# Merge gates of a hybrid decoder: seven products of block sums instead of eight block products

## The chip, the cores and the metric

The kernel runs on one core of a Trainium2 chip. Times are microseconds (us) of device time for one call; a call computes both layers. The median of three runs of the kernel before is 2449.65 us (2448.92 to 2451.15).

## The reference, cut to what matters

Two layers, 1024 prompt tokens and 8 sample tokens (T = 1032), model width 1024. Each layer makes four branch outputs y of width 384 and merges them:

```python
h = rms_norm(x, norm_g)                                   # (T, 1024)
proj_b = einsum('bsne,ned->bsnd', branches, w_branch)     # 4 x (384 -> 1024)
gates  = sigmoid(h @ w_merge)                             # 1024 -> 4 * 1024
merged = sum(gates * proj_b, over the 4 branches)
x = x + merged @ w_out
```

`h @ w_merge` is the largest product of the layer. Everything is float32 in and out.

## The kernel before, in words

Activations lie feature-major: 128 features by T tokens a tile, eight tiles k = 0..7 for the model width. Each fp32 operand is kept as a high and a low part (fp32r), and a product is three matmuls: high x high, high x low, low x high (`mm_cols`, L178, L181, L182). The normalised input is `hh` and `hl`. A weight tile arrives raw (`wr`), ScalarE (ACT) copies its high part `wh` (L154), GpSimd (POOL) subtracts to get the low part `wl` (L156); that is `split_w`. `wr` has 2 buffers, `wh` and `wl` 4 each, of up to 8 x 128 columns.

The merge of a layer (L884 to L923) loops over the four branches `bi`, over eight output tiles `m` and over three chunks of 344 tokens. For each it issues 24 gate matmuls (k = 0..7) and 9 matmuls of the branch projection, all of 344 columns. Then VectorE (DVE) scales the gate by 1/rms (`rr`, L917), ACT takes tanh (L918), DVE multiplies with the projection out of PSUM (L920, L922), and from the second branch on POOL adds it to the sum `mg` (L923). Per layer this is 4 x 8 x 3 x 33 = 3168 matmuls, 6336 in both. After it `mg` is split into parts (`split_m`, L881, L882) for the output projection (L983 on).

A scheduler of the framework puts each engine's instructions in order. Each engine then runs its own list strictly in order and waits on semaphores. Pools with a fixed number of buffers set when a tile can be written again. "Tag" below is such a set of buffers: `slot` has 31.

Of the kernel before, what the change touches and what calls it, by code (L numbers as in the profile page):

```python
# [7 lines left out]
F32 = mybir.dt.float32  # L8
F32R = mybir.dt.float32r
# [4 lines left out]
P = 128  # L14
# [6 lines left out]
NCH = 3  # L21
MIX = 384
# [10 lines left out]
def kernel(ctx: ExitStack, tc: tile.TileContext, i, o, c):  # L33
# [5 lines left out]
    sl = ctx.enter_context(tc.tile_pool(name="sl", bufs=31))  # L39
# [33 lines left out]
    # ---- loads are held back until the products a given number of tiles before them have been issued  # L73
# [23 lines left out]
    # ---- constants  # L97
# [17 lines left out]
    # ---- cache copies, cut in pieces that go out between the weights  # L115
# [32 lines left out]
    # ---- weights: raw tile -> high and low parts  # L148
    def split_w(shape, dmas):
        raw = wp.tile(list(shape), F32, tag="wr", name="wr", bufs=2)  # L150
# [4 lines left out]
        lo = wp.tile(list(shape), F32R, tag="wl", name="wl", bufs=4)  # L155
        pool.tensor_tensor(lo, raw, hi.bitcast(F32), op=ALU.subtract)  # L156
        return hi, lo

# [3 lines left out]
    def w_std(src, kt):  # L162
        r = split_w([P, kt, P], [(lambda t: t, src)])
        copy_piece()
        return r

    def w_pair(l, c0, j):
        r = split_w([P, KT, P], [
            (lambda t: t[:, :, 0:64], win_cols(l, c0 + 64 * j, 64)),
            (lambda t: t[:, :, 64:128], win_cols(l, c0 + 192 + 64 * j, 64))])  # L170
        copy_piece()
        return r

# [13 lines left out]
    # short products that go out one lot after each chunk of long ones  # L187
# [10 lines left out]
    # ---- the normalised input is kept as (x * g) in two parts; 1/rms is applied to what the products give  # L198
# [75 lines left out]
    for l in range(2):  # L274
        # ================= projections with rotary positions
# [21 lines left out]
        # ================= layer constants  # L297
# [42 lines left out]
        # ================= token-major projections  # L340
        def tm_group(srcs, kk, consumer):
            N = sum(n for _, n in srcs)
            ws = []
            for k0 in range(0, KT, kk):
# [7 lines left out]
                copy_piece()  # L352
# [18 lines left out]
        def tm_v(srcs, off):  # L371
            """V rows of two attentions: to memory, to the caches"""
# [9 lines left out]
            tm_group(srcs, 4, ev)  # L382
# [27 lines left out]
        tm_group([(C_V, MIX)], 2, ev_c)  # L410
# [17 lines left out]
        # ================= branch C: layer norm and spatial mix  # L428
# [82 lines left out]
        def pv(s, nk, vs, out):  # L511
            """vs[kb][h]: [128 keys, 64]; out: psum [128, 128] for the two heads."""
# [15 lines left out]
        # ---- branch B, prompt  # L528
# [35 lines left out]
        # ---- decode of both attention branches  # L564
        class Decode:
# [14 lines left out]
            def scores(self, j, q, k):  # L580
                """q, k: [128, 8], two heads of the new tokens"""
# [20 lines left out]
        def decode_finish(D, O):  # L602
# [47 lines left out]
            def values(j0):  # L650
                """two parts, one per head"""
# [33 lines left out]
        yscr = [dscr(f"yscr{l}_{n}", [3, P, T]) for n in range(3)]  # L685
# [5 lines left out]
        # ================= branch A  # L691
# [38 lines left out]
        # ---- branch D, prompt  # L730
# [85 lines left out]
        # ---- gates of B  # L816
# [13 lines left out]
        # ---- weights of the dilated groups from their maxima and denominators  # L830
# [48 lines left out]
        def split_m(m, ch):
            cs = slice(ch * CH, (ch + 1) * CH)  # L880
            act.activation(mh[m][:, cs], mg[m][:, cs], AF.Copy)  # L881
            dve.tensor_tensor(ml[m][:, cs], mg[m][:, cs], mh[m].bitcast(F32)[:, cs], op=ALU.subtract)  # L882

        order = (2, 3, 1, 0)  # L884
        for bi, n in enumerate(order):
            yh, yl = [], []
            yy = ynext
            for j in range(3):
                t = yy[j]
                th, tl = slot(f"yh{n}{j}", F32R), slot(f"yl{n}{j}", F32R)  # L890
                act.activation(th, t, AF.Copy)
                dve.tensor_tensor(tl, t, th.bitcast(F32), op=ALU.subtract)
                yh.append(th)
                yl.append(tl)
            for m in range(KT):
                ms = slice(m * P, (m + 1) * P)
                if n == 1:
                    wv = i["w_branch"][l, n, :, ms].rearrange("(h j p) m -> h p j m", h=2, p=64)
                    wpj = split_w([P, 3, P], [(lambda t: t[0:64], wv[0]), (lambda t: t[64:128], wv[1])])
                else:  # L900
                    wpj = split_w([P, 3, P], [(lambda t: t,
                                               i["w_branch"][l, n, :, ms].rearrange("(j p) m -> p j m", p=P))])
                wg = w_std(i["w_merge"][l, :, n * DM + m * P:n * DM + (m + 1) * P].rearrange("(k p) m -> p k m", p=P), KT)
                if bi == 0:
                    mg[m] = slot(f"mg{m}")
                if bi == 0 and m == 0:
                    ynext = yD
                if m == 4 and bi in (1, 2):
                    ynext = load_y(order[bi + 1])
                for ch in range(NCH):  # L910
                    cs = slice(ch * CH, (ch + 1) * CH)
                    pg = pacc()
                    mm_chunk(pg, wg, KT, hh, hl, ch)
                    pp = pacc()
                    mm_chunk(pp, wpj, 3, yh, yl, ch)
                    t = ctmp("th")
                    dve.tensor_tensor(t, pg[:, :CH], rr[:, cs], op=ALU.mult)  # L917
                    act.activation(t, t, AF.Tanh, scale=0.5)  # L918
                    if bi == 0:
                        dve.scalar_tensor_tensor(mg[m][:, cs], t, 1.0, pp[:, :CH], op0=ALU.add, op1=ALU.mult)  # L920
                    else:
                        dve.scalar_tensor_tensor(t, t, 1.0, pp[:, :CH], op0=ALU.add, op1=ALU.mult)  # L922
                        pool.tensor_tensor(mg[m][:, cs], mg[m][:, cs], t, op=ALU.add)  # L923
# [14 lines left out]
        def final_block(n, last):  # L938
            """final norm of one block of tokens, back to token-major"""
# [81 lines left out]
def _constants():  # L1021
    """Tables that depend on shapes alone: rotary factors by position, masks, the identity."""
# [35 lines left out]
```

## Time and profile before

| | |
|---|---|
| median of three runs | 2449.65 us |
| span of the profiled execution | 2449.6 us |
| busy: PE / DVE / ACT / POOL | 99% / 37% / 29% / 34% |
| granted TensorE clock, mean | 0.994 |
| DMA | 235.82 MB, mean 96 GB/s |

The span is the time from the first to the last instruction of the profiled execution, and it stands at the median of the timed runs, so a sum against the span is one against the median. PE is TensorE's matmuls; its busy share counts overlapping matmuls once.

### The profile page before, as it was taken

The page shows a single profiled execution, that of the slowest core. Times are in us where ns is not written, and L with a number is a line of the kernel's source. Part 1 is how long each engine was busy: PE and PEld are TensorE (multiplying, and loading weights), DVE is VectorE, ACT ScalarE, POOL GpSimd, SP SyncE. Part 2 cuts the span into 40 slices and gives each one's busy share as a digit, 9 for nine tenths or more (in the row PEclk, how much of TensorE's full clock was granted, in tenths as well). Part 3 has the DMA queues.
Part 4 walks back from the last instruction along what each step waited for, and adds up shares of the span by engine and source line. Part 5 has one row for each costly group of instructions (what it writes and reads, how often), then busy time and mean ns, then how long its engine had stood idle before and what let it go on. Part 6 is the DMA issues. An engine that isn't in the chain of part 4 may idle for free.

```text
span 2449.6 us, 38865 instructions
## 1 busy us (share of the span) xinstructions
PE 2423.4 (99%) x15896; PEld 2305.9 (94%) x15896; DVE 894.5 (37%) x1930; ACT 705.7 (29%) x1526; POOL 841.5 (34%) x556
## 2 busy tenths in 40 slices
PE   8999999999999999999999999999999999999999
PEld 7998889889999999999999988898899999999998
DVE  4456534435312221224333554443352122212253
ACT  6234432322212221224323254313222121212243
POOL 3342235342222343444433413343223233444330
PEclk9999999999999999999999999999999999999999
DMA  7252216242322222223442523342352221222232
GB/s 240 87 150 80 71 45 184 64 134 81 94 69 65 92 65 95 65 68 120 146 146 73 147 66 80 100 147 60 100 137 67 70 91 56 93 65 69 76 97 99
DMA packets 295963, 235.82 MB, mean 96 GB/s; under 512 B 52757, under 2 KB 279697, under 8 KB 293417
## 3 DMA queue, kind: packets, MB, share of 16 engines
q1 hardware_dynamic: 267952, 206.25, 28.1%
q10 hardware_dynamic: 27832, 27.10, 3.9%
q8 instruction: 125, 2.05, 0.4%
q14 instruction: 54, 0.43, 0.1%
HBM read 192.35 MB, written 76.47 MB: 110 GB/s over the span
## 4 chain that ended last, share of the span: by engine, by line
PE 94%; DVE 2%; DMA 1%; ACT 1%; POOL 1%; issue 0%; ACTq 0%; SPq 0%; POOLq 0%; DVEq 0%
PE acc L181 26%; PE acc L178 26%; PE acc L182 26%; PE sc L500 3%; PE acc L360 2%; PE acc L363 2%; PE acc L364 2%; PE ms L522 2%; PE ms L517 2%; PE ms L662 1%; DMA qs<-dk 1%; PE ms L467 0%; DVE ml L882 0%; DVE dk L291 0%; POOL qs L290 0%
## 5 line engine op out<-in xcount | busy, mean ns | idle before, releaser
L156 POOL TENSOR_TENSOR wl<-wr,wh 128x384 fp32r<-128x384 f32 (+2 forms) x228 | 465.9, 2045 | 864.5 <-ACT wh L154 764.7
L181 PE MATMUL acc<-h1l,wh 128*128 128x344 f32 x1584 | 513.7, 324 | 0.0
L178 PE MATMUL acc<-h0h,wh 128*128 128x344 f32 x1584 | 512.7, 324 | 0.4 <-ACT wh L154 0.3
L181 PE MATMUL acc<-h0l,wh 128*128 128x344 f32 x1584 | 513.1, 324 | 0.0
L182 PE MATMUL acc<-h0h,wl 128*128 128x344 f32 x1584 | 512.6, 324 | 0.0
L178 PE MATMUL acc<-h1h,wh 128*128 128x344 f32 x1584 | 512.3, 323 | 0.1
L182 PE MATMUL acc<-h1h,wl 128*128 128x344 f32 x1584 | 511.0, 323 | 0.0
L154 ACT ACTIVATE wh<-wr 128x384 fp32r<-128x384 f32 (+2 forms) x228 | 205.1, 901 | 440.5 <-PE acc L181 403.2
L181 PEld LDWEIGHTS acc<-h0l,wh 128*128 128x128 f32 x1584 | 300.3, 190 | 11.4 <-issue 10.6
L181 PEld LDWEIGHTS acc<-h1l,wh 128*128 128x128 f32 x1584 | 299.8, 189 | 11.0 <-issue 10.7
L917 DVE TENSOR_TENSOR th<-acc,rr 128x344 f32<-128x344 f32 x192 | 99.0, 516 | 572.9 <-PE acc L182 572.9
L178 PEld LDWEIGHTS acc<-h0h,wh 128*128 128x128 f32 x1584 | 300.0, 189 | 5.3 <-issue 3.4
L178 PEld LDWEIGHTS acc<-h1h,wh 128*128 128x128 f32 x1584 | 299.5, 189 | 4.6 <-issue 3.4
L182 PEld LDWEIGHTS acc<-h0h,wl 128*128 128x128 f32 x1584 | 299.8, 189 | 2.5 <-issue 2.0
L182 PEld LDWEIGHTS acc<-h1h,wl 128*128 128x128 f32 x1584 | 299.5, 189 | 2.5 <-issue 2.0
L918 ACT ACTIVATE th<-th 128x344 f32<-128x344 f32 x192 | 94.3, 491 | 525.2 <-DVE th L917 525.2
L923 POOL TENSOR_TENSOR mg<-mg,th 128x344 f32<-128x344 f32 x144 | 138.0, 958 | 309.8 <-DVE th L922 309.8
L181 PE MATMUL acc<-yl,wh 128*128 128x344 f32 x576 | 184.3, 320 | 0.0
L182 PE MATMUL acc<-yh,wl 128*128 128x344 f32 x576 | 184.2, 320 | 0.0
L178 PE MATMUL acc<-yh,wh 128*128 128x344 f32 x576 | 184.2, 320 | 0.0
L181 PE MATMUL acc<-ml,wh 128*128 128x344 f32 (+3 forms) x384 | 123.2, 322 | 0.6 <-DVE ml L882 0.5
L182 PE MATMUL acc<-mh,wl 128*128 128x344 f32 (+3 forms) x384 | 122.0, 320 | 0.0
(268 smaller groups left out, 3305.3 us busy)
## 6 DMA issues: line engine op xcount, KB each, us to landing
wr<-in_w_merge_dram SPq DMA_DIRECT2D x64, 512.0 KB
out_dram<-in_cache_dil_kv_dram SPq DMA_DIRECT2D x128, 255.9 KB
wr<-in_w_in_dram SPq DMA_DIRECT2D x60, 512.0 KB
y<-yscr SPq DMA_DIRECT2D x18, 516.0 KB
wr<-in_w_branch_dram SPq DMA_DIRECT2D x48, 192.0 KB
wr<-in_w_in_dram SPq DMA_DIRECT2D x32, 256.0 KB
wr<-in_w_out_dram SPq DMA_DIRECT2D x16, 512.0 KB
out_dram<-in_cache_dil_kv_dram SPq DMA_DIRECT2D x16, 511.0 KB
```

Of the source, the lines that this page charges most:

```text
L154: act.activation(hi, raw, AF.Copy)
L156: pool.tensor_tensor(lo, raw, hi.bitcast(F32), op=ALU.subtract)
L178: mm = pe.matmul(ps[:, :n], hi[:, k], xh[k][:, cs], start=(k == 0), stop=False)
L181: pe.matmul(ps[:, :n], hi[:, k], xl[k][:, cs], start=False, stop=False)
L182: pe.matmul(ps[:, :n], lo[:, k], xh[k][:, cs], start=False, stop=(k == kt - 1))
L360: mm = pe.matmul(ps[:M, :N], lh, hi[:, k % kk], start=(k == 0), stop=False)
L363: pe.matmul(ps[:M, :N], ll, hi[:, k % kk], start=False, stop=False)
L364: pe.matmul(ps[:M, :N], lh, lo[:, k % kk], start=False, stop=(k == KT - 1))
L500: pe.matmul(ps[h][:, :nk], qs[h], ks[h], start=True, stop=True)
L917: dve.tensor_tensor(t, pg[:, :CH], rr[:, cs], op=ALU.mult)
L918: act.activation(t, t, AF.Tanh, scale=0.5)
L923: pool.tensor_tensor(mg[m][:, cs], mg[m][:, cs], t, op=ALU.add)
```

## The change

Two output tiles m, m+1 (one group q of four) and the two halves of k make a 2 x 2 block matrix of weights, a11, a12, a21, a22. Tokens go in two halves of 516 (`HT`), each cut in two quarters of 258 (`QT`); with the two halves of k these are a 2 x 2 block matrix of inputs. The gate of a group is then seven block products in place of eight (Strassen's scheme in Winograd's form): four sums of weight blocks s1..s4 (DVE, L935, tag `ws` with 2 buffers), four sums of input blocks once per half (`inputs_t`), and sums of products, partly by accumulating in PSUM (`X`, `Y`, `Z`), partly on DVE from copies `u` (ACT, L1027). Each of the seven weight blocks is split into high and low: five low parts on POOL, two (s3, s4) on DVE, all at L162.

Each half runs through all four branches and all weights, so merge and branch weights are loaded and split twice. The first two groups of the first branch of each half stay plain (`NPLAIN`). Weight tiles are now 4 x 128 columns with 8 buffers for `wr`, `wh`, `wl`; loads and splits outside the merge go in two pieces. The sums `mg` of the first half go to memory and come back for the output projection.

```diff
-    sl = ctx.enter_context(tc.tile_pool(name="sl", bufs=31))
+    sl = ctx.enter_context(tc.tile_pool(name="sl", bufs=32))
...
-        hi = wp.tile(list(shape), F32R, tag="wh", name="wh", bufs=4)
+        return split_r(raw, shape)
+    def split_r(raw, shape, eng=pool):
+        hi = wp.tile(list(shape), F32R, tag="wh", name="wh", bufs=8)
         act.activation(hi, raw, AF.Copy)
-        pool.tensor_tensor(lo, raw, hi.bitcast(F32), op=ALU.subtract)
+        lo = wp.tile(list(shape), F32R, tag="wl", name="wl", bufs=8)
+        eng.tensor_tensor(lo, raw, hi.bitcast(F32), op=ALU.subtract)
...
+        def summed(a, b, op):
+            t = wp.tile([P, 4, P], F32, tag="ws", name="ws", bufs=2)
+            dve.tensor_tensor(t, a, b, op=op)
+            return t
...
+                    def close(m):
+                        for c in range(2):
+                            cs = slice(c * QT, (c + 1) * QT)
+                            out = mg[q][:, m, cs] if bi == 0 else gt[m][:, cs]
+                            dve.scalar_tensor_tensor(out, gt[m][:, cs], 1.0, pps[m][c], op0=ALU.add, op1=ALU.mult)
+                        if bi:
+                            pool.tensor_tensor(mg[q][:, m], mg[q][:, m], gt[m], op=ALU.add)
...
+                    X, Y, Z = pscore()[:, :QT], pmisc()[:, :QT], pmisc()[:, :QT]
+                    block(X, w_(a11), b_(0, 0), True, True)
+                    p1 = kept(X)
+                    project(0, 0)
+                    s1 = summed(a21, a22, ALU.add)
+                    s2 = summed(s1, a11, ALU.subtract)
+                    ws2, ws1 = w_(s2), w_(s1)
+                    block(X, ws2, t_(1), False)
+                    u1 = kept(X)
+                    block(Z, w_(a12), b_(1, 0), True)
+                    dve.tensor_tensor(gt[0][:, :QT], p1, Z, op=ALU.add)
+                    s3 = summed(a11, a21, ALU.subtract)
+                    block(X, w_(s3, dve), t_(2), False, True)
+                    u2 = kept(X)
+                    project(0, 1)
+                    block(Y, ws1, t_(0), True)
+                    dve.tensor_tensor(gt[1][:, QT:], u2, Y, op=ALU.add)
+                    s4 = summed(a12, s2, ALU.subtract)
+                    project(1, 0)
+                    block(X, w_(a22), t_(3), False)
+                    scale(1, 0, X)
+                    gate(1, 0, 1)
+                    block(Y, w_(s4, dve), b_(1, 1), False)
+                    dve.tensor_tensor(gt[0][:, QT:], u1, Y, op=ALU.add)
+                    dve.tensor_tensor(gt[1][:, QT:], gt[1][:, QT:], rr[:, c0 + QT:c0 + HT], op=ALU.mult)
+                    gate(1, 1, 2)
+                    dve.tensor_tensor(gt[0], gt[0], rr[:, c0:c0 + HT], op=ALU.mult)
+                    gate(0)
+                    project(1, 1)
+                    close(0)
+                    close(1)
```

`block` is 12 matmuls of 258 columns, `project` 9 of them, `scale` a DVE multiply out of PSUM (L985), `gate` a tanh on ACT, `kept` a copy on ACT.

What this makes of the order of DVE and POOL in the merge is shown at two places of layer 0. Before, DVE has two instructions per chunk in the third branch, both with one operand in PSUM (`acc`):

```order
L917 TENSOR_TENSOR th_7637<-acc_7602,rr_520 128x344
L922 SCALAR_TENSOR_TENSOR th_7637<-th_7637,acc_7627 128x344
L917 TENSOR_TENSOR th_7677<-acc_7642,rr_520 128x344
L922 SCALAR_TENSOR_TENSOR th_7677<-th_7677,acc_7667 128x344
L917 TENSOR_TENSOR th_7717<-acc_7682,rr_520 128x344
L922 SCALAR_TENSOR_TENSOR th_7717<-th_7717,acc_7707 128x344
```

Of the change, the same place, one group whose X is `sc_8652`; `ws` are sums of weight blocks, `wr`, `wh`, `wl` weight parts, `ms` and `sc` PSUM:

```order
L935 TENSOR_TENSOR ws_8942<-wr_8853,wr_8855 128x512
L1046 TENSOR_TENSOR g1_8642<-u_8751,ms_8653 128x258
L1054 TENSOR_TENSOR g1_8642<-g1_8642,rr_533 128x258
L162 TENSOR_TENSOR wl_8946<-ws_8942,wh_8944 128x512
L935 TENSOR_TENSOR ws_8985<-wr_8859,ws_8901 128x512
L995 SCALAR_TENSOR_TENSOR g1_8642<-g1_8642,acc_8834 128x258
L935 TENSOR_TENSOR ws_9122<-wr_9079,wr_9081 128x512
L985 TENSOR_TENSOR g1_8642<-sc_8652,rr_533 128x258
L1053 TENSOR_TENSOR g0_8641<-u_8714,ms_8653 128x258
L995 SCALAR_TENSOR_TENSOR g1_8642<-g1_8642,acc_8785 128x258
L1056 TENSOR_TENSOR g0_8641<-g0_8641,rr_533 128x516
L162 TENSOR_TENSOR wl_9024<-ws_8985,wh_9022 128x512
```

Behind these come one more sum (`ws_9124`), the two L995 that close `g0_8641`, and an L1040 for the next group: 16 instructions per group, eight of which (the four L935, the two L162, L1054, L1056) read both inputs from SBUF. The weight work on DVE is one or two groups ahead of the matmuls. The first row, `ws_8942`, takes a buffer of `ws` that `ws_8899` held, so it waits for POOL's `wl_8909`.

POOL before, from the end of the third branch into the fourth:

```order
L923 TENSOR_TENSOR mg0_6276<-mg0_6276,th_8494 128x344
L156 TENSOR_TENSOR wl_8678<-wr_8673,wh_8676 128x384
L923 TENSOR_TENSOR mg0_6276<-mg0_6276,th_8534 128x344
L156 TENSOR_TENSOR wl_8684<-wr_8680,wh_8682 128x1024
L923 TENSOR_TENSOR mg1_6407<-mg1_6407,th_8588 128x344
L923 TENSOR_TENSOR mg1_6407<-mg1_6407,th_8628 128x344
```

POOL of the change, around the same group as DVE's rows above:

```order
L997 TENSOR_TENSOR mg1_6768<-mg1_6768,g0_8432 128x516
L162 TENSOR_TENSOR wl_8887<-wr_8882,wh_8885 128x384
L162 TENSOR_TENSOR wl_8905<-ws_8901,wh_8903 128x512
L162 TENSOR_TENSOR wl_8909<-ws_8899,wh_8907 128x512
L162 TENSOR_TENSOR wl_8927<-wr_8859,wh_8925 128x512
L162 TENSOR_TENSOR wl_8992<-wr_8987,wh_8990 128x384
L162 TENSOR_TENSOR wl_9006<-wr_8857,wh_9004 128x512
L997 TENSOR_TENSOR mg2_6959<-mg2_6959,g1_8642 128x516
L162 TENSOR_TENSOR wl_9090<-wr_9077,wh_9088 128x512
L997 TENSOR_TENSOR mg2_6959<-mg2_6959,g0_8641 128x516
```

Nine instructions per group in place of five per output tile. The add of `g0` (last row, and the first one for the group before) stands ahead of the splits of the next group's first projection weight, s2 and s1.

## Rows read from the trace of the kernel before

**Rows 1.** The page: span, engines' busy time, granted clock by fortieths.
```profile
span 2449.6 us, 38865 instructions
PE 2423.4 (99%) x15896; PEld 2305.9 (94%) x15896; DVE 894.5 (37%) x1930; ACT 705.7 (29%) x1526; POOL 841.5 (34%) x556
PEclk9999999999999999999999999999999999999999
```

**Rows 2.** Busy time by stretch; (x) counts instructions, last columns clock, DMA share, GB/s.
```profile
core 0: us, PE busy (x) PEld busy (x) DVE busy (x) ACT busy (x) POOL busy (x), PEclk, DMA share, GB/s
641.00:1145.00 504.00, 504.00 (x3198) 503.82 (x3196) 125.97 (x218) 115.42 (x192) 185.43 (x138) 1.00 0.24 75
1860.00:2356.00 496.00, 495.68 (x3143) 494.99 (x3142) 128.11 (x222) 115.27 (x193) 179.66 (x136) 1.00 0.24 75
780.00:880.00 100.00, 100.00 (x638) 100.00 (x637) 19.56 (x38) 18.87 (x31) 39.70 (x32) 1.00 0.27 87
1341.70:1364.40 22.70, 22.70 (x192) 22.70 (x191) 11.04 (x22) 4.73 (x9) 6.87 (x3) 1.00 0.61 165
1145.00:1242.00 97.00, 96.70 (x612) 96.17 (x612) 39.57 (x57) 32.39 (x60) 40.91 (x30) 1.00 0.51 150
```

**Rows 3.** Groups by line and shape: busy us, mean ns of one, idle before.
```profile
L363 PE MATMUL acc<-wh,h1l 128*128 128x256 f32 x128 | 36.6, 286 | 0.0
L156 POOL TENSOR_TENSOR wl<-wr,wh 128x1024 fp32r<-128x1024 f32 x156 | 384.2, 2465 | 538.3 <-ACT wh L154 471.8 <-PE acc L364 49.5 <-DMA vscr<-vn 16.9
L156 POOL TENSOR_TENSOR wl<-wr,wh 128x384 fp32r<-128x384 f32 x64 | 65.0, 1016 | 307.7 <-ACT wh L154 274.4 <-PE acc L182 33.3
L701 POOL TENSOR_TENSOR z<-z,rr 128x1032 f32<-128x1032 f32 x6 | 14.5, 2415 | 35.7 <-DVE z L699 25.8 <-PE acc L178 9.9
L502 DVE CUSTOM_DVE_ANT_0 s<-sc,band 128x256 f32<-128x256 f32 x128 | 49.4, 421 | 81.6 <-PE sc L500 68.9 <-ACT pt L519 12.0
L154 ACT ACTIVATE wh<-wr 128x1024 fp32r<-128x1024 f32 x156 | 165.0, 1058 | 180.4 <-PE acc L181 151.4 <-DMA wr<-in_w_in_dram 16.5 <-DMA cD<-in_cache_dil_kv_dram 3.7
L918 ACT ACTIVATE th<-th 128x344 f32<-128x344 f32 x192 | 94.3, 491 | 525.2 <-DVE th L917 525.2
```

**Rows 4.** Single lines: shortest, median and longest duration in ns.
```profile
L156 POOL TENSOR_TENSOR wl<-wr,wh x228: 1004/2392/4567, 14.6 to 2388.2; 128x384 fp32r<-128x384 f32 x64, 128x1024 fp32r<-128x1024 f32 x46, 128x768 fp32r<-128x768 f32 x4
L923 POOL TENSOR_TENSOR mg<-mg,th x144: 916/927/1929, 771.7 to 2348.9; 128x344 f32<-128x344 f32 x144
L882 DVE TENSOR_TENSOR ml<-mg,mh x48: 499/504/2710, 1132.3 to 2352.5; 128x344 fp32r<-128x344 f32 x48
L892 DVE TENSOR_TENSOR yl<-y,yh x18: 1221/1239/2593, 630.7 to 2220.8; 128x1032 fp32r<-128x1032 f32 x18
L917 DVE TENSOR_TENSOR th<-acc,rr x192: 501/517/519, 641.0 to 2340.6; 128x344 f32<-128x344 f32 x192
```

**Rows 5.** Timelines of DVE and of POOL, 886.5 to 894.5 us.
```profile
889.23 4.46 DVE L892 TENSOR_TENSOR yl<-y,yh 128x1032 fp32r<-128x1032 f32 x2 [0.63 <-ACT yh L891]
...
888.32 2.41 POOL L156 TENSOR_TENSOR wl<-wr,wh 128x1024 fp32r<-128x1024 f32 x1 [1.23 <-ACT wh L154]
890.68 1.92 POOL L923 TENSOR_TENSOR mg<-mg,th 128x344 f32<-128x344 f32 x1
```

**Rows 6.** Who waited for whom: us in total, times, longest.
```profile
POOL wl L156 <- ACT wh L154: 764.7, 144, 16.5
DVE th L917 <- PE acc L182: 572.9, 178, 3.6
```

**Rows 7.** DMA issues, KB each.
```profile
wr<-in_w_merge_dram SPq DMA_DIRECT2D x64, 512.0 KB
wr<-in_w_branch_dram SPq DMA_DIRECT2D x48, 192.0 KB
wr<-in_w_branch_dram SPq DMA_DIRECT2D x32, 96.0 KB
```

More of the change, by code (lines that the diff above doesn't have):

```diff
@@ L21 @@
 NCH = 3
+HT = T // 2
+QT = T // 4
+NPLAIN = 2
 MIX = 384
@@ L149, in split_w, with both @@
     def split_w(shape, dmas):
-        raw = wp.tile(list(shape), F32, tag="wr", name="wr", bufs=2)
+        raw = wp.tile(list(shape), F32, tag="wr", name="wr", bufs=8)
         for sel, src in dmas:
             load(sel(raw), src, 4)
-        hi = wp.tile(list(shape), F32R, tag="wh", name="wh", bufs=4)
+        return split_r(raw, shape)
+    def split_r(raw, shape, eng=pool):
+        hi = wp.tile(list(shape), F32R, tag="wh", name="wh", bufs=8)
         act.activation(hi, raw, AF.Copy)
-        lo = wp.tile(list(shape), F32R, tag="wl", name="wl", bufs=4)
-        pool.tensor_tensor(lo, raw, hi.bitcast(F32), op=ALU.subtract)
+        lo = wp.tile(list(shape), F32R, tag="wl", name="wl", bufs=8)
+        eng.tensor_tensor(lo, raw, hi.bitcast(F32), op=ALU.subtract)
         return hi, lo
+    def both(parts, kk):
+        return [(hi[:, k], lo[:, k]) for hi, lo in parts for k in range(kk)]
     def win_cols(l, c0, n):
@@ L162, in w_std @@
     def w_std(src, kt):
-        r = split_w([P, kt, P], [(lambda t: t, src)])
+        r = both([split_w([P, 4, P], [(lambda t: t, src[:, k0:k0 + 4])]) for k0 in range(0, kt, 4)], 4)
         copy_piece()
@@ L167, in w_pair @@
     def w_pair(l, c0, j):
-        r = split_w([P, KT, P], [
-            (lambda t: t[:, :, 0:64], win_cols(l, c0 + 64 * j, 64)),
-            (lambda t: t[:, :, 64:128], win_cols(l, c0 + 192 + 64 * j, 64))])
+        s0, s1 = win_cols(l, c0 + 64 * j, 64), win_cols(l, c0 + 192 + 64 * j, 64)
+        r = both([split_w([P, 4, P], [
+            (lambda t: t[:, :, 0:64], s0[:, k0:k0 + 4]),
+            (lambda t: t[:, :, 64:128], s1[:, k0:k0 + 4])]) for k0 in (0, 4)], 4)
         copy_piece()
@@ L174, in mm_cols @@
     def mm_cols(ps, w, kt, xh, xl, cs, first):
-        hi, lo = w
         n = cs.stop - cs.start
         for k in range(kt):
-            mm = pe.matmul(ps[:, :n], hi[:, k], xh[k][:, cs], start=(k == 0), stop=False)
+            hi, lo = w[k]
+            mm = pe.matmul(ps[:, :n], hi, xh[k][:, cs], start=(k == 0), stop=False)
             if k == 0 and first:
                 mark(mm)
-            pe.matmul(ps[:, :n], hi[:, k], xl[k][:, cs], start=False, stop=False)
-            pe.matmul(ps[:, :n], lo[:, k], xh[k][:, cs], start=False, stop=(k == kt - 1))
+            pe.matmul(ps[:, :n], hi, xl[k][:, cs], start=False, stop=False)
+            pe.matmul(ps[:, :n], lo, xh[k][:, cs], start=False, stop=(k == kt - 1))
     def mm_chunk(ps, w, kt, xh, xl, ch):
@@ L351, in tm_group @@
                 ws.append(split_w([P, kk, N], dmas))
-                copy_piece()
+                if k0 % (2 * kk) == 0:
+                    copy_piece()
             for n in list(range(8)) + [8]:
@@ L381, in ev @@
                     act.dma_start(vscr[n * P:(n + 1) * P, off:off + 256], vdst(n))
-            tm_group(srcs, 4, ev)
+            tm_group(srcs, 2, ev)
             for nm, c0 in (("swa_p", 0), ("dil_p0", 128), ("dil_p1", 256), ("dil_p2", 384)):
@@ L409, in ev_c @@
             dve.bn_aggr(lnmv[:M, n], lnst[:M, n])
-        tm_group([(C_V, MIX)], 2, ev_c)
+        tm_group([(C_V, MIX)], 1, ev_c)
         qB.append(rope_tile(w_pair(l, S_Q, 2), "qB2"))
@@ L683, in ev_mul @@
             return f
-        yscr = [dscr(f"yscr{l}_{n}", [3, P, T]) for n in range(3)]
+        yscr = [dscr(f"yscr{l}_{n}", [3, P, T]) for n in range(4)]
         for j in range(3):
@@ L859, with load_y @@
         gate_a(2)
-        def load_y(n):
-            r = [dec([P, T], f"y{n}{j}") for j in range(3)]
+        def load_y(n, half):
+            r = [dec([P, T], f"y{n}{j}")[:, :HT] for j in range(3)]
             for j in range(3):
-                load(r[j], yscr[n][j], 1)
+                load(r[j], yscr[n][j][:, half * HT:(half + 1) * HT], 1)
             return r
-        ynext = load_y(2)
+        ynext = load_y(2, 0)
         for j in range(3):
@@ L873 @@
             pool.tensor_tensor(yD[j], OD[j], sgs[j], op=ALU.mult)
-        mg = [None] * KT
-        mh, ml = [None] * KT, [None] * KT
[L879 to L923, printed above, removed]
@@ new lines, with inputs_t @@
+            store_later(1, yscr[3][j], yD[j])
+        mscr = dscr(f"mscr{l}", [KT, P, HT])
+        def inputs_t(c0):
+            th, tl = [], []
+            for k in range(4):
+                x1 = tp.tile([P, HT], F32, tag="s", name="x1", bufs=2)
+                x2 = tp.tile([P, HT], F32, tag="pt", name="x2", bufs=2)
+                cs = slice(c0, c0 + HT)
+                dve.tensor_tensor(x1, hh[k][:, cs].bitcast(F32), hl[k][:, cs].bitcast(F32), op=ALU.add)
+                dve.tensor_tensor(x2, hh[k + 4][:, cs].bitcast(F32), hl[k + 4][:, cs].bitcast(F32), op=ALU.add)
+                tf = sl.tile([P, 4, QT], F32, tag="slot", name="tf")
+                b11, b12, b21, b22 = x1[:, :QT], x1[:, QT:], x2[:, :QT], x2[:, QT:]
+                dve.tensor_tensor(tf[:, 0], b12, b11, op=ALU.subtract)
+                dve.tensor_tensor(tf[:, 1], b22, tf[:, 0], op=ALU.subtract)
+                dve.tensor_tensor(tf[:, 2], b22, b12, op=ALU.subtract)
+                dve.tensor_tensor(tf[:, 3], b21, tf[:, 1], op=ALU.subtract)
+                h_ = sl.tile([P, 4, QT], F32R, tag="slot", name=f"th{k}")
+                l_ = sl.tile([P, 4, QT], F32R, tag="slot", name=f"tl{k}")
+                act.activation(h_, tf, AF.Copy)
+                pool.tensor_tensor(l_, tf, h_.bitcast(F32), op=ALU.subtract)
+                th.append(h_)
+                tl.append(l_)
+            return th, tl
@@ new lines, in block @@
+        def block(ps, w, x, first, marked=False):
+            for k in range(4):
+                hi, lo = w[k]
+                xh_, xl_ = x(k)
+                mm = pe.matmul(ps, hi, xh_, start=(first and k == 0), stop=False, skip_group_check=not first)
+                if marked and k == 0:
+                    mark(mm)
+                pe.matmul(ps, hi, xl_, start=False, stop=False, skip_group_check=not first)
+                pe.matmul(ps, lo, xh_, start=False, stop=(k == 3), skip_group_check=not first)
@@ L924 @@
+        mh, ml = [None] * KT, [None] * KT
         for m in range(KT):
             mh[m], ml[m] = slot(f"mh{m}", F32R), slot(f"ml{m}", F32R)
-        for ch in range(NCH):
+        for half in range(2):
+            hs = slice(half * HT, (half + 1) * HT)
             for m in range(KT):
-                split_m(m, ch)
+                if half == 0:
+                    src = dec([P, T], "m0")[:, :HT]
+                    load(src, mscr[m], 1)
+                else:
+                    src = mg[m // 2][:, m % 2]
+                act.activation(mh[m][:, hs], src, AF.Copy)
+                dve.tensor_tensor(ml[m][:, hs], src, mh[m].bitcast(F32)[:, hs], op=ALU.subtract)
```

86 lines of the change are left out of this document (85 added, 1 removed).

## The prediction, on record before the changed kernel ran

> **What bounds the kernel now.** I read the page first: PE is busy 2423.4 of 2449.6 us and its granted clock stands in the top tenth in every fortieth of the span [rows 1]. No other engine passes 37%. The stretches by stage come next. The two merges (about 641 to 1145 us and 1860 to 2356 us) have PE busy without a gap, at clock 1.00; there POOL is busy 37%, DVE 25%, ACT 23% [rows 2]. The waits say the same from the other side: POOL waited 764.7 us for the ACT copies that become possible when PE frees a buffer, DVE 572.9 us for PE [rows 6]. So in the merge every engine waits for PE, and a merge costs its number of matmuls times their pitch. In the stretch 780 to 880 us PE issued 638 matmuls of 344 columns in 100.00 us, 156.7 ns each. The stretch 1341.7 to 1364.4 us holds 192 matmuls of 256 columns in 22.70 us, 118.2 ns each [rows 2, 3]. That is the same cost per column with the weight load included, so shorter products lose nothing: 258 columns cost 118.2 + 2 x (156.7 - 118.2)/88 = 119.1 ns.
>
> **What PE is spared.** Removed: 6336 matmuls of 344 columns, 6336 x 156.7 ns = 993 us. Added, by the loops: 2 layers x 2 halves x 16 groups = 64 groups. 56 are in the new form, with 7 x 12 gate matmuls and 4 x 9 of the projection, 120 x 119.1 ns = 14.3 us each. 8 are plain, 96 + 36 = 132 matmuls, 15.7 us each. Sum 800 + 126 = 926 us. PE gains 67 us, and if it stays the bound the time is about 2383 us before small losses.
>
> **What the other engines get.** I cost one group of a later branch, 14.3 us of PE, from rows, by straight lines between the sizes that the rows show.
> - POOL: a 384-column split 1.02 us and a 1024-column one 2.39 us [rows 3, 4] give 1.29 us for 512. An add of 344 takes 0.93 us and a product of 1032 2.415 us, so an add of 516 takes 1.30 us. Nine instructions: 5 x 1.29 + 2 x 1.02 + 2 x 1.30 = 11.1 us.
> - DVE, both inputs in SBUF: 0.50 us alone for 344 and 1.24 us for 1032 (medians of `ml` and `yl`) [rows 4], so 0.68 for 512 or 516 and 0.41 for 258. Eight instructions: 7 x 0.68 + 0.41 = 5.2 us.
> - DVE, one input in PSUM: 0.42 us for 256 (L502) [rows 3]. Eight: 3.4 us.
> - ACT: 1.06 us per 1024 and 0.49 per 344 [rows 3] make about 0.6 for 512; seven splits, two of 384, three copies and three tanh are about 8 us.
>
> Each fits into 14.3 us alone. But DVE and POOL don't run alone. `ml` takes 504 ns as a rule and up to 2710 ns; `wl` on POOL up to 4567 against 2392; while L917, whose one input is in PSUM, never takes over 519 [rows 4]. The timeline at 889 us shows why. POOL's 1024-column split runs from 888.32 to 890.73; `yl` starts at 889.23, and two of them need 4.46 us instead of 2.48; POOL's add behind them starts at 890.68 and needs 1.92 instead of 0.93 [rows 5]. A DVE instruction with two SBUF inputs and a POOL instruction exclude each other; the later one stands until the other has ended. Of the three that queued here (`yl`, add, `yl`, alone 1.24 + 0.93 + 1.24 = 3.41) the chain from 890.73 to 893.69 took 2.96 us: each handover saves some 0.15 us of start-up. The Trainium skill says the same on its page "SBUF — State Buffer", section "Who interferes with whom": the port pair shared by VectorE and GpSimd is an exclusive lock for a whole instruction, against a DVE instruction with two SBUF inputs too. It speaks against this change: by it without any saving one group needs 11.1 + 5.2 = 16.3 us of the lock, more than PE's 14.3, and 48 such groups would cost 96 us more than PE. By the row, with half of the 16 possible handovers saving 0.15, it is 15.1 us and 38 us.
>
> In the merge before, this never mattered: DVE's two instructions per chunk both have an input in PSUM. The change brings eight exclusive DVE instructions per group into a stage where POOL is 11.1/14.3 = 78% busy.
>
> **The loop.** Order makes it worse than the sum. In DVE's list a group's first sum of the next group's blocks (the L935 for s3) needs a `ws` buffer that POOL's split of s1 frees. From there DVE works through its list to the two L995 that close `g0`: 5.2 us with two SBUF inputs plus seven from PSUM, 2.9 us, together 8.1. Then POOL must add `g0` (1.30), split the projection weight (1.02), s2 and s1 (2 x 1.29), 4.9 us, before DVE's next first sum may start. 8.1 + 4.9 = 13.0 us if nothing collides, below PE's 14.3. But POOL's five other instructions of the group (a12, second projection weight, a22, add of `g1`, next a11: 3 x 1.29 + 1.02 + 1.30 = 6.2 us) fall into DVE's 8.1 us, where they exclude five of its eight instructions. Bounds: none in the way 13.0 (PE stays the bound), all of it 19.2. DVE's PSUM instructions cover some of it and back-to-back DVE instructions may keep POOL out, so I take a little over half, 3.4 us: 16.4 us per group, 2.1 us more than PE's, for the 48 groups of branches two to four: +101 us. PE then stands before the matmuls of the s4 block (they wait for the L1046 behind that sum) or before a projection product. Groups of the first branch have no POOL adds: lock sum below 14, no loss.
>
> **Smaller terms.** At the start of each half `inputs_t` puts 24 exclusive DVE instructions (8 x 0.68 + 16 x 0.41 = 12 us) and four POOL splits of 1032 (9.7 us) under two plain groups of 31.4 us, where POOL has another 14.5 us of weight splits and the next groups' work: 36 us and more of lock. Part can go out earlier; I take 6 us a half, 24 in all (0 to 45). At the 12 other changes of branch the `yl` parts add three exclusive instructions of 0.68 to the loop, less what PE's shortage hides: 1.3 us, 16 in all. Splitting the sums for `w_out` after the last group: 2 us a layer. Halving the weight tiles elsewhere adds about 0.2 us of POOL per tile in stages where POOL mostly waits for ACT [rows 6], hidden; without that cover 156 tiles would cost 30 us.
>
> Transfers: merge weights 64 x 512 KB and branch weights 48 x 192 + 32 x 96 KB [rows 7] (the latter two issues a tile) once more, 45 MB over 1000 us, +45 GB/s on the 75 shown, DMA share from 0.24 to about 0.4. The stretch at 1145 to 1242 us moves 150 GB/s at 0.51 with PE busy 96.7 of 97.0 [rows 2], so they hide.
>
> Sum: 2449.6 - 67 + 101 + 24 + 16 + 4 = 2528 us; I say 2525.
>
> **The rivals.**
> - PE stays the bound (faster): weight work runs up to eight buffers ahead, so DVE and POOL collide harmlessly. For it: every wait in the merge before ends at PE [rows 6], and the loop without collisions is 13.0 us. Against: 16.3 us of lock per group. It decides when fewer than 1.3 of the 6.2 us stand in DVE's way. 2383 + 10 for starts: 2393 (2380 to 2410).
> - The lock's sum alone, no loop: 15.1 us a group, +38 us; with starts and changes of branch about 2383 + 38 + 25 = 2446 (2415 to 2470). For it: order could be slack enough that POOL always has other work; against: POOL's list is fixed.
> - All collisions count, or loads come late into the loop (a raw tile is freed by DVE's last sum of it, so a late DVE issues loads late): 18.5 us a group, +200 us: 2630 (2590 to 2680).
>
> **How the numbers follow.** Forecast (2470 to 2590) 0.60, PE-bound 0.18, lock sum 0.17, worse 0.05. A measurement of this kernel tells 0.2% (5 us) from no change. PE-bound is faster; of the lock sum I count 0.07 faster, 0.04 the same, 0.06 slower. Faster 0.25, same 0.04, slower 0.71. The range for 8 in 10 takes in the forecast and the lock sum and leaves out most of PE-bound and of worse: 2415 to 2585; the forecast's own range is 2470 to 2590.
>
> **What the profile after would show.** Right: matmuls of 258 columns at a pitch of 118 to 121 ns where they run on; PE busy share down to about 93%, its idle time in the merge, released by DVE; DVE's L935 and L162 with means of 1 us or more against 0.68 alone, while L985 and L995 stay near 0.42; POOL's 512-column splits above 1.3 us; a group about 16.4 us from one L1046 to the next. Wrong: PE without gaps in the merge (the loop has slack that I don't see), a pitch above 125 ns (shorter products cost more than the 256-column row says), waits of ACT or DVE for `wr` loads (transfers), or long PE gaps at the starts of halves alone.

## The result, and the profile of the changed kernel

The changed kernel takes 2580.8 us (median of 4 runs, 2574.48 to 2583.13) against 2449.9 us before, a ratio of the mean times of 1.0529 (95% interval 1.0514 to 1.0544): 131 us slower, at the upper end of the forecast's own range.

The page of the profiled execution, span, engines and clock by fortieths (answers to [rows 1]):
```profile
span 2578.0 us, 45026 instructions
PE 2413.3 (94%) x17336; PEld 2267.1 (88%) x17336; DVE 1451.8 (56%) x2610; ACT 978.1 (38%) x2234; POOL 1256.9 (49%) x936
PEclk9999999999999989999999999999989999999999
```
PE has 10 us less busy time than before and a span 128 us longer. DVE and POOL are far from full over the span, and the clock dips in two fortieths, one in each merge. The stretches show where; the first lies in the first branch, the second holds nine groups of branches two to four, the last two a start of a half (answers to [rows 2]):
```profile
core 0: us, PE busy (x) PEld busy (x) DVE busy (x) ACT busy (x) POOL busy (x), PEclk, DMA share, GB/s
680.00:700.00 20.00, 20.00 (x169) 20.00 (x169) 9.54 (x14) 7.66 (x15) 10.49 (x9) 1.00 0.37 112
742.00:896.00 154.00, 137.99 (x1100) 133.30 (x1100) 114.25 (x150) 67.66 (x143) 110.03 (x84) 1.00 0.38 113
654.00:663.00 9.00, 0.00 (x0) 0.00 (x0) 8.97 (x10) 2.52 (x4) 6.87 (x5) 0.78 0.30 110
663.00:666.00 3.00, 2.93 (x14) 2.93 (x15) 2.11 (x6) 1.70 (x2) 1.47 (x2) 0.52 0.49 136
```
Where PE runs on, 169 matmuls of 258 columns take 20.00 us, 118.3 ns each: the shorter products cost what was forecast. In 742 to 896 us PE stands 16 of 154 us with the clock at full. At a start of a half it stands for 9 us and then works at a granted clock of 0.52.

The groups by line in 742 to 896 us (busy us, mean ns, idle before; answers to [rows 3, 4]):
```profile
L162 POOL TENSOR_TENSOR wl<-wr,wh 128x512 fp32r<-128x512 f32 x27 | 39.6, 1465 | 12.3 <-ACT wh L160 11.9
L162 POOL TENSOR_TENSOR wl<-ws,wh 128x512 fp32r<-128x512 f32 x19 | 25.6, 1366 | 0.0
L162 POOL TENSOR_TENSOR wl<-wr,wh 128x384 fp32r<-128x384 f32 x19 | 21.1, 1110 | 16.3 <-ACT wh L160 16.3
L997 POOL TENSOR_TENSOR mg<-mg,g 128x516 f32<-128x516 f32 x19 | 27.2, 1434 | 15.4 <-DVE g L995 14.4 <-PE sc L926 1.0
...
L935 DVE TENSOR_TENSOR ws<-wr 128x512 f32<-128x512 f32 x18 | 24.7, 1370 | 20.2 <-POOL wl L162 20.2
L162 DVE TENSOR_TENSOR wl<-ws,wh 128x512 fp32r<-128x512 f32 x18 | 21.9, 1215 | 2.1 <-ACT wh L160 2.1
L1056 DVE TENSOR_TENSOR g<-g,rr 128x516 f32<-128x516 f32 x9 | 12.1, 1342 | 0.1
L995 DVE SCALAR_TENSOR_TENSOR g<-g,acc 128x258 f32<-128x258 f32 x36 | 14.1, 413 | 0.3 <-ACT g L989 0.2
L1046 DVE TENSOR_TENSOR g<-u,ms 128x258 f32<-128x258 f32 x9 | 3.8, 421 | 14.6 <-ACT u L1027 14.6
```
The DVE lines with both inputs in SBUF (L935, L162, L1056) take 1.2 to 1.4 us on average where 0.68 was worked out for one alone; those with an input in PSUM (L995, L1046) stay at 0.41 to 0.42. That split was forecast. The extremes, over the whole run, show it without an average (shortest, median, longest ns):
```profile
L935 DVE TENSOR_TENSOR ws<-wr x112: 673/1447/1774, 656.3 to 2444.7; 128x512 f32<-128x512 f32 x112
L1056 DVE TENSOR_TENSOR g<-g,rr x56: 680/1560/1793, 706.6 to 2470.8; 128x516 f32<-128x516 f32 x56
L995 DVE SCALAR_TENSOR_TENSOR g<-g,acc x192: 407/411/427, 733.3 to 2475.0; 128x258 f32<-128x258 f32 x192
```
The shortest are the 0.68 us of the estimate; the longest are one POOL instruction longer. Waits in 742 to 896 us (us in total, times, longest), and, in the last two rows, PE's over the run:
```profile
DVE ws L935 <- POOL wl L162: 20.2, 9, 4.6
POOL wl L162 <- ACT wh L160: 28.2, 15, 2.4
POOL mg L997 <- DVE g L995: 14.4, 10, 2.2
PE acc L978 <- DVE g L995: 9.6, 7, 1.8
...
PE acc L189 <- DVE g L985: 35.9, 4, 10.8
PE acc L189 <- DVE g L995: 22.0, 6, 8.2
```
In the groups PE waits mostly for DVE's L995 to free an accumulator (9.6 of its 16 us, in seven waits, before a projection product). The last two rows are the starts of the halves and of `w_out`: ten waits, 58 us in all.

### The profile page after: what moved, and what is told of

Same layout as the page of the kernel before. It is cut to its first block, busy times and chain, and to the rows that moved or that the text cites. A ratio compares the mean times of both kernels' runs of the same rounds, so it can differ in the third digit from the quotient of the medians.

```text
span 2578.0 us, 45026 instructions
## 1 busy us (share of the span) xinstructions
PE 2413.3 (94%) x17336; PEld 2267.1 (88%) x17336; DVE 1451.8 (56%) x2610; ACT 978.1 (38%) x2234; POOL 1256.9 (49%) x936
## 5 line engine op out<-in xcount | busy, mean ns | idle before, releaser
L162 POOL TENSOR_TENSOR wl<-wr,wh 128x512 fp32r<-128x512 f32 (+1 forms) x528 | 697.2, 1329 | 744.1 <-ACT wh L160 692.1
L160 ACT ACTIVATE wh<-wr 128x512 fp32r<-128x512 f32 (+1 forms) x528 | 308.0, 594 | 287.5 <-PE acc L192 137.5
L189 PE MATMUL acc<-h0h,wh 128*128 128x344 f32 (+1 forms) x944 | 306.9, 326 | 26.5 <-DVE g L985 17.1
L189 PE MATMUL acc<-h1h,wh 128*128 128x344 f32 (+1 forms) x944 | 305.2, 323 | 27.2 <-DVE g L985 18.8
L192 PE MATMUL acc<-h0l,wh 128*128 128x344 f32 (+1 forms) x944 | 307.7, 326 | 0.4 <-POOL h0l L225 0.4
L193 PE MATMUL acc<-h0h,wl 128*128 128x344 f32 (+1 forms) x944 | 306.5, 325 | 0.0
L192 PE MATMUL acc<-h1l,wh 128*128 128x344 f32 (+1 forms) x944 | 306.3, 325 | 0.0
L193 PE MATMUL acc<-h1h,wl 128*128 128x344 f32 (+1 forms) x944 | 304.7, 323 | 0.0
L978 PE MATMUL acc<-yhl,wh 128*128 128x258 f32 x768 | 222.6, 291 | 39.6 <-DVE g L995 38.6
L979 PE MATMUL acc<-yhl,wh 128*128 128x258 f32 x768 | 218.9, 285 | 5.2 <-DVE yhl L949 4.6
L935 DVE TENSOR_TENSOR ws<-wr 128x512 f32<-128x512 f32 x112 | 149.2, 1332 | 123.0 <-POOL wl L162 122.7
L980 PE MATMUL acc<-yhl,wl 128*128 128x258 f32 x768 | 216.6, 282 | 0.0
L189 PEld LDWEIGHTS acc<-h1h,wh 128*128 128x128 f32 x944 | 182.0, 193 | 31.1 <-DVE g L985 19.2
L922 PE MATMUL sc<-th,wh 128*128 128x258 f32 x672 | 192.5, 287 | 14.5 <-ACT u L1027 14.1
```

The lines of the kernel that those rows point to most:

```text
L162: eng.tensor_tensor(lo, raw, hi.bitcast(F32), op=ALU.subtract)
L189: mm = pe.matmul(ps[:, :n], hi, xh[k][:, cs], start=(k == 0), stop=False)
L192: pe.matmul(ps[:, :n], hi, xl[k][:, cs], start=False, stop=False)
L193: pe.matmul(ps[:, :n], lo, xh[k][:, cs], start=False, stop=(k == kt - 1))
L922: mm = pe.matmul(ps, hi, xh_, start=(first and k == 0), stop=False, skip_group_check=not first)
L935: dve.tensor_tensor(t, a, b, op=op)
```

## The experiments

Each ran against the kernel before on the same chip; that stood at 2449.6 to 2451.1 us in the three series, and a difference to the changed kernel is one to its 2580.8 us of the first measurement. Four of them came first, each cutting one suspected cost. Times are medians of 4 runs (5 for `all_spread`).

**Splits of two sums to DVE (`s12_dve`).**
```diff
-                    ws2, ws1 = w_(s2), w_(s1)
+                    ws2, ws1 = w_(s2, dve), w_(s1, dve)
```


> The low parts of the weight sums s1 and s2 are computed by DVE instead of POOL; nothing else changes. Theory of the prediction (exclusive turns plus the loop through the two ws buffers): a group's exclusive work falls by 2 x (1.29 - 0.68) = 1.2 us and POOL's last piece of the loop (2.6 us) is gone, so a group of branches two to four falls from 16.6 us to 14.6 to 15.3, the kernel from 2580 to about 2495 us (2470 to 2520). Rival 'sum of the turns alone, no loop': 1.2 us a group, 2580 - 56 x 1.2 = 2513. Rival 'DVE simply has too much of its own work, POOL does not matter': DVE gets 1.36 us more a group and the kernel gets slower, 2640 or more.

Measured: 2511.6 us (ratio to before 1.0258, 1.0240 to 1.0275), 69 us faster than the changed kernel. That is what the sum of the turns says (2513), and it lies in the loop's range too (2470 to 2520), so the run doesn't tell the two apart. From one L1046 to the next a group takes 15.2 us on average over the four halves, where the changed kernel takes 16.5. Giving the busier engine more work made the kernel faster, so "DVE has too much of its own work" falls.

**All big splits of the new groups on DVE (`all_dve`).** The same edit for a11, a12 and a22 too.

> All weight splits of the new groups except those of the projection are done by DVE (five more per group than in the changed kernel); POOL keeps the projection splits and the gate adds. Theory of the prediction: exclusive work per group falls by 5 x (1.29 - 0.68) = 3 us to about 12, and DVE's own work rises to 8.6 + 3.4 = 12.0 us, both below PE's 14.3, so PE is nearly the bound again in these groups: about 2460 us (2440 to 2490), with the starts of the halves as the remaining loss. Rival 'DVE simply has too much work': 56 x 3.4 = 190 us more, about 2770. Rival 'late weight loads': no change, 2570 to 2590.

Measured: 2467.7 us (1.0079, 1.0063 to 1.0094). The stretch that answers to the one above, and two DVE lines in it:
```profile
742.00:880.00 138.00, 138.00 (x1153) 138.00 (x1152) 134.29 (x207) 72.86 (x151) 56.92 (x40) 1.00 0.48 141
```
```profile
L162 DVE TENSOR_TENSOR wl<-wr,wh 128x512 fp32r<-128x512 f32 x28 | 27.4, 978 | 0.7 <-PE acc L980 0.6
...
L1056 DVE TENSOR_TENSOR g<-g,rr 128x516 f32<-128x516 f32 x10 | 7.3, 727 | 0.0
```
PE stands no more in the groups, though DVE is busy 97%: L1056 is down from 1342 to 727 ns.

**Without the gate adds (`no_add`).** The two lines of POOL's L997 are removed.

> POOL's adds of the gates of branches two to four into the merge sum are left out (so the sum keeps the first branch only). Theory of the prediction: 2 x 1.30 us of exclusive POOL work per group goes, one add of it lies in the loop; groups of branches two to four fall from 16.6 to about 14.5 us, 48 x 2.1 = 100 us: about 2480 us (2460 to 2510). Rival 'sum of the turns alone': the same size within 15 us. Rival 'POOL is off the path, since it is only half busy': 2570 to 2590.

Measured: 2472.4 us (1.0093, 1.0077 to 1.0108). So POOL's adds cost time although POOL is busy 71% in the stretch above. The loop's range (2460 to 2510) and the sum of the turns (the same within 15 us) both allow the number.

**The T matrices in four parts (`spread`).**
```diff
-                        tt = inputs_t(c0)
+                        tt = ([], [])
...
                             close(m)
+                            inputs_t(c0, (2 * q + m,), *tt)
```


> The T matrices of a half are made in four parts, one behind each of the four plain weight tiles of the half, instead of all ahead of the first; nothing else changes. Theory of the prediction (24 exclusive DVE instructions and four wide POOL splits stand ahead of the DVE instruction that frees PE's accumulators, and the clock falls after the wait): of the four starts, with 9 to 16 us of PE's waiting each and some 2 to 4 us at half clock, most goes: about 2540 us (2525 to 2560). Rival 'the work at the start is bound by the turns of DVE and POOL whatever its order': the wait moves to the first new group, 2570 to 2585.

Measured: 2545.2 us (1.0390, 1.0375 to 1.0406), 36 us faster. In 640 to 680 us PE is busy 39.93 us where the changed kernel had 13.97 + 16.93 = 30.9.

**Both together (`all_spread`).**

> Both edits that won time: the weight splits of the new groups on DVE, and the T matrices made in four parts behind the plain weight tiles. If the two losses are separate (turns of DVE and POOL in the groups, and the queue at the starts), the gains add: 2580.8 - 113 - 36 = 2432 us (2422 to 2442), below the kernel before. Rival 'they share one resource': with DVE as full as it is then, the T parts delay the groups behind them, 2445 to 2460.

Measured: 2421.8 us (0.9878, 0.9856 to 0.9900), 1.2% below the kernel before and 10 us below the sum of the two gains. Its page, then one stretch, then its longest wait of PE in the merges:
```profile
span 2420.0 us, 44976 instructions
PE 2374.3 (98%) x17336; PEld 2252.4 (93%) x17336; DVE 1515.0 (63%) x2890; ACT 988.3 (41%) x2234; POOL 898.3 (37%) x656
```
```profile
742.00:860.00 118.00, 118.00 (x986) 118.00 (x986) 116.17 (x178) 62.27 (x129) 46.34 (x32) 1.00 0.46 136
```
```profile
PE acc L189 <- DVE g L994: 18.6, 4, 4.8
```
What is left in the merges is up to 4.8 us at the end of each half, where PE waits for the last L994 (L995 before the edit).

**Plain groups only (`all_plain`).** `plain = True`, and no T matrices.

> Halves, weights loaded twice, tiles of 4 x 128 and products of 258 columns as in the changed kernel, but every group is plain: no sums of weights, no T matrices, no kept copies. PE's matmuls cost 6336 x 4/3 x 119.1 - 6336 x 156.7 ns = 13 us more than before, the stages outside the merges took 10 us more in the changed kernel, and DVE has no instruction with two SBUF inputs in the merges but the yhl splits. Theory of the prediction: PE is the bound, 2449.6 + 13 + 10 = 2473 us (2460 to 2485). Rival 'the loss is in the halves, the double loads or the short products': 2520 or more.

Measured: 2478.0 us (1.0114, 1.0091 to 1.0137). In the first merge PE is busy in all 507.00 of 507.00 us:
```profile
641.00:1148.00 507.00, 507.00 (x4235) 506.98 (x4233) 134.46 (x283) 157.77 (x285) 295.84 (x241) 1.00 0.49 149
```
The halves, the second loads (149 GB/s here), the short products and the smaller weight tiles cost 27 us together. Each merge takes 506 to 507 us from its first matmul to the first of `w_out`, 499.5 before; that is 14 us, about the 13 of the products of 258 columns, and the other 13 lie in the stages outside the merges. The rest of the changed kernel's loss is the new groups and the T matrices.

**The reverse: s3 and s4 to POOL (`s34_pool`).** `w_(s3)` and `w_(s4)` without `dve`.

> The low parts of s3 and s4 go from DVE (75% busy in these groups) to POOL (71% busy), the reverse of the first experiments. Theory of the prediction: exclusive work per group grows by 2 x (1.29 - 0.68) = 1.2 us, 56 x 1.2 = 68 us: 2650 us (2625 to 2690). Rival 'DVE has too much work of its own': DVE is relieved of 1.4 us a group, 2500 to 2550. Rival 'balance of the two engines does not matter': 2570 to 2590.

Measured: 2570.9 us (1.0487, 1.0464 to 1.0511), 10 us faster than the changed kernel: a miss for every theory but the flat one. The stretch that answers to 742 to 896 us, and POOL's waits in it by line:
```profile
742.00:894.00 152.00, 138.33 (x1101) 134.58 (x1101) 107.01 (x133) 66.80 (x142) 139.92 (x101) 0.99 0.38 115
```
```profile
L162 POOL TENSOR_TENSOR wl<-ws,wh 128x512 fp32r<-128x512 f32 x38 | 52.0, 1381 | 8.8 <-ACT wh L160 8.8
...
L997 POOL TENSOR_TENSOR mg<-mg,g 128x516 f32<-128x516 f32 x18 | 29.5, 1643 | 3.0 <-DVE g L995 3.0
```
POOL stood idle 44 us of the stretch in the changed kernel and 12 us here. The longer turns filled time in which POOL had waited for results of DVE and of ACT's copies behind DVE's sums, so they cost nothing: the turns were not in use all the time. The sum of the turns had said 68 us more, so that sum alone does not set the time.

**A third `ws` buffer (`ws3`).** `bufs=2` to 3 for `ws`, 8 to 7 for the raw tiles.

> Three buffers for the sums of blocks instead of two, and seven raw weight tiles instead of eight to make room. The prediction's loop (DVE's first sum of the next group waits for a ws buffer that POOL's split frees): the exclusive turns stood unused for some 1.6 us a group, and this buffer should give most of that back, 50 to 80 us: about 2510 us (2495 to 2535). Rival 'only the sum of the turns counts, the wait for the buffer is a sign of it': 2560 to 2585.

Measured: 2565.4 us (1.0467, 1.0439 to 1.0495), 15 us faster. The wait of L935 for POOL's split stays at 19.9 us in 742 to 894 us. A group takes 16.0 us where it took 16.5. A third buffer takes little of that wait away, so this buffer alone is not what holds the groups. The seven raw tiles may have cost part of the gain: L935 waits 2.4 us for a load in this stretch, which it never does in the changed kernel.

**Added adds, both inputs in SBUF (`extra_sbuf`), or one in PSUM (`extra_psum`).** `all_plain` with
```diff
+        def extra():
+            for _ in range(4):
+                dve.tensor_tensor(xo_, xr_, xs_, op=ALU.add)
```
four times a group; `xr_` is a piece of `rr` in SBUF, or `xp_` in PSUM in the second kernel.

> The kernel with plain groups only (2478 us), and in each group 16 added DVE adds of 512 columns that nothing uses, both inputs in SBUF. DVE's own work is then 16 x 0.68 + 8 x 0.42 = 14.3 us of the group's 15.9 us of PE. Theory of the prediction (a DVE instruction with two SBUF inputs and a POOL instruction exclude each other): 10.9 us of DVE and 9.8 us of POOL in the 48 groups of branches two to four, less 16 handovers of 0.15, is 18.3 us, 2.4 more than PE's: 2478 + 115 = 2593 us (2555 to 2640). Rival 'no exclusion, DVE is only slower by its own waits': 2470 to 2500.

> The same 16 added DVE adds per group, with one of the two inputs taken from a PSUM bank that stands unused in this kernel. Theory of the prediction: these instructions do not exclude POOL's, each takes about 0.6 to 0.7 us and PE stays the bound: 2478 us (2470 to 2495), the adds at one duration. Rival 'the number of DVE instructions is what costs': as long as the run with both inputs in SBUF.

Measured: 2662.8 us (1.0864, 1.0841 to 1.0887) and 2481.3 us (1.0119, 1.0096 to 1.0141). The added line in each, first for `extra_sbuf`, then for `extra_psum` (ns, then first and last start), and a stretch of the latter's merge with its DVE splits L960, both inputs in SBUF (busy us, mean ns):
```profile
L948 DVE TENSOR_TENSOR xo__6514<-rr,xs__6513 x512: 645/691/2904, 62.7 to 758.6; 128x512 f32<-128x512 f32 x171
```
```profile
L948 DVE TENSOR_TENSOR xo__6514<-sc,xs__6513 x512: 648/691/694, 579.5 to 1099.6; 128x512 f32<-128x512 f32 x171
```
```profile
780.00:1100.00 320.00, 320.00 (x2674) 320.00 (x2673) 288.93 (x504) 99.00 (x176) 187.68 (x155) 1.00 0.50 151
```
```profile
L960 DVE TENSOR_TENSOR yhl<-y,yhl 128x516 fp32r<-128x516 f32 x15 | 16.1, 1100 | 0.0
```
With one input in PSUM none of the 512 adds took more than 694 ns, while POOL was busy 59% beside them and PE all the time. In the same stretch the L960, 0.68 us by the estimate for one alone, took 1.10 us on average: POOL held up these and not the adds. The first kernel did not do what it was made for: with inputs ready early, its adds were put ahead, at 62.7 to 758.6 us, and lengthened the stages before the merge, so its time says nothing of the groups. What it shows is the line's spread: the same add, alone just as long (median 691), takes up to 2904 ns.

**The rest of POOL's work (`proj_dve`, `a11_pool`).** From `all_spread`: the projection splits to DVE as well, or a11's split back to POOL.

> The fastest version so far (2421.8 us), and the two projection splits of a new group on DVE as well, so that POOL has only the gate adds there. Exclusive work falls by another 2 x (1.02 - 0.55) = 0.9 us a group, but DVE's own comes to 12.0 + 1.1 = 13.1 us of PE's 14.3, plus the yhl splits. If PE is the bound in the groups already, nothing is won: 2415 to 2430. Rival 'the turns still cost something': 2400 to 2415. Rival 'DVE is full': 2435 or more.

> The fastest version so far (2421.8 us) with the split of a11 back on POOL. Exclusive work rises by 0.6 us a group to about 12.6, DVE's own falls to 11.3. If PE is the bound with room to spare: 2415 to 2430, perhaps a few us less where DVE is late at the ends of the halves. Rival 'each turn of POOL costs': 0.6 us x 56 = 34 us more, 2440 to 2460.

Measured: 2420.4 us (0.9880, 0.9855 to 0.9904) and 2426.5 us (0.9907, 0.9885 to 0.9928): neither differs from `all_spread` (0.9856 to 0.9900) by more than the intervals. PE is the bound there, and there is room on both sides.

## Why the prediction came out as it did

The sign was right, and so was the first half of the mechanism: DVE's instructions with two SBUF inputs and POOL's hold each other up, and PE stands for it. The time was 56 us above the number. Most of that is the starts of the halves, a term taken too small, and the second half of the mechanism, the loop through the `ws` buffer, is not borne out. By the terms of its sum, against the profiled spans (2578.0 - 2449.6 = 128.4 us):

| term | forecast | measured | from |
|---|---|---|---|
| PE's matmuls | -67 | -67 | worked out, not measured by itself: 118.3 ns a matmul above gives -73, 507.00/4224 = 120.0 in `all_plain` -60, the forecast's 119.1 lies between |
| new groups, changes of branch in them | +101 + 16 | +112 | below |
| starts and ends of halves, `w_out` | +24 + 4 | +69 | what is left; most of it PE's ten waits above, 58 us |
| stages outside the merges | 0 | +14.5 | the first merge begins 8.9 us later (first matmul at 645.76, before 636.91), 4.3 more between the merges, 1.3 behind, with `w_out` counted from its first matmul |

*Shorter products cost the same per column:* right. *PE's gain of 67 us is there:* `all_spread` shows part of it: its merges take 480 us each, from the first matmul to the first of `w_out`, where the kernel before takes 499.5.

*The groups:* right in size. From first to last L1046 of a half are 13 groups:
```profile
L1046 DVE TENSOR_TENSOR g<-u,ms x14: 409/424/425, 700.2 to 910.9; 128x258 f32<-128x258 f32 x14
L1046 DVE TENSOR_TENSOR g<-u,ms x14: 408/423/425, 979.4 to 1195.8; 128x258 f32<-128x258 f32 x14
```
With the two halves of the second layer (211.5 and 217.0 us) these are 855.6 us for 52 groups, 16.5 each; at PE's 14.3 they were 743.6. That 16.4 came so near is in part luck: 3.4 of the 6.2 us of POOL's work in the loop was a choice between bounds of 13.0 and 19.2.

*Exclusive turns as a reason:* shown, though not as the whole of it. Work moved off POOL onto the busier DVE made the groups faster twice, the first time by what the turns give (69 us), the second until PE was the bound (113 us); and the add with an input in PSUM was never held up, the same add from SBUF was, and so was L960 beside the unheld adds. Against the turns as the only reason stands `s34_pool`, which added turns and cost nothing. The Trainium skill has the rule on "SBUF — State Buffer", section "Who interferes with whom" (a DVE instruction with two SBUF inputs contends with a GpSimd one that reads SBUF, one with at most one SBUF input, outside the two-port modes, does not); the trace agrees with both halves, 2904 ns against 694 at the longest.

*The loop through the `ws` buffer* is the step that failed. It gave 16.4 us for a group, near what was measured, but another buffer gave back 15 us, not 50 to 80 (with one raw tile less beside it). The splits of s1 and s2 on DVE gave 1.3 us a group, which fits the turns' 1.2 and the loop's 1.3 to 2 alike. The turns alone make the same number for the stretch: POOL's 46 splits of 512, 19 of 384 and 19 adds and DVE's 69 instructions of 512 or 516 and 9 of 258 in 742 to 896 us come to 46 x 1.29 + 19 x 1.02 + 19 x 1.30 + 69 x 0.68 + 9 x 0.41 = 154 us of 154. That this sum is a floor does not hold either: with s3 and s4 on POOL it is 164 us in a stretch of 152. Laid over each other, the instructions of the two engines cover 139 of the 154 us, and 146.5 of the 152; so neighbours overlap, an engine's own by some 0.08 us (659.80 + 1.48 against 661.20 below), and a handover saves some too (an L935 of `s34_pool`, 805.16 to 806.90 us, ends 0.55 us after POOL's split, 805.09 to 806.35, where 0.68 is its time alone). The rest of each stretch, 15 and 5.5 us, neither holds the turn; that each then waits for what the other makes is read from the waits, not tested. Which of these mutual waits costs how much was not told apart.

*The starts of halves* are the term that was mis-sized: 28 us forecast with the ends and `w_out`, 69 measured as what is left, most of the error. I had seen 36 us of exclusive work there and taken 6 a half, "part can go out earlier". The order put most of it ahead of the L985 that frees PE's accumulators: at the first start 19 of the 24 DVE instructions of `inputs_t` and two of its four splits on POOL. DVE and PE at the first start:
```profile
652.43 2.88 DVE L900 TENSOR_TENSOR x<-h0h,h0l 128x516 f32<-128x516 f32 x1
...
657.24 2.64 DVE L906 TENSOR_TENSOR tf<-x,x 128x258 f32<-128x258 f32 x1
659.80 1.48 DVE L935 TENSOR_TENSOR ws<-ws,wr 128x512 f32<-128x512 f32 x1
661.20 1.48 DVE L905 TENSOR_TENSOR tf<-x,tf 128x258 f32<-128x258 f32 x1
662.60 0.75 DVE L985 TENSOR_TENSOR g<-acc,rr 128x258 f32<-128x258 f32 x2
```
```profile
653.69 0.28 PE L980 MATMUL acc<-yhl,wl 128*128 128x258 f32 x1
663.07 0.58 PE L189 MATMUL acc<-h0h,wh 128*128 128x258 f32 x1 [9.10 <-DVE g L985]
663.45 0.42 PE L192 MATMUL acc<-h0l,wh 128*128 128x258 f32 x1
663.66 0.42 PE L193 MATMUL acc<-h0h,wl 128*128 128x258 f32 x1
```
An L906 of 258 columns, 0.42 us where nothing holds it, took 2.64; PE had used up its accumulators at 653.97 us and stood 9.1 us for the L985 at the end of this queue. `spread` gave back 36 us of it.

*Stages outside the merges:* forecast as hidden, 14.5 us. `all_plain`, without T matrices, has 13 of it; no run undid the smaller tiles there alone, so their share is open. *Transfers:* hidden, as forecast; `all_plain` loads at 149 GB/s with PE never standing.

Of the rivals, "PE stays the bound" is what the kernel becomes when DVE does the splits and the T matrices are spread (2421.8 us against its 2393, above its range of 2380 to 2410; 18.6 us of waits at the ends of halves and 10 us in the stages outside the merges are left). "The lock's sum alone" described `ws3` better than the loop did; `s12_dve` and `no_add` fit both, `s34_pool` neither.

## What to carry to other kernels

Add up DVE's instructions with two SBUF inputs and POOL's as one resource, per group of work, before comparing with PE. The sum is a warning and not the time (164 us of turns went into 152 us here). Where it is near the bound, give the work to the engine that does it in the shorter turn, even if it is the busier one (1.29 us on POOL, 0.68 on DVE). A batch of preparations should not stand in an engine's queue ahead of the instruction that frees PE's buffers: cut it in parts behind such instructions. A saving in PE's matmuls (67 us here) is had only when what prepares the operands fits under the shorter time.

## What the runs showed of the hardware

DVE's add of 512 columns takes 691 ns (median) whether one of its inputs is in PSUM or both are in SBUF; what differs is the longest beside POOL, 694 against 2904 ns. After the 9.1 us in which PE stood, the granted clock was 0.52 in the next 3 us (the 1.2 GHz level), with matmuls of 258 columns 0.21 to 0.22 us apart instead of 0.12: a stall cost more than its length.
